# Grouped-query attention on one core: five of sixteen exps on VectorE in a fixed pattern, with three shared score slots

## The chip, the core and the metric

The kernel runs on one core of a Trainium2 chip. The metric is the device time of one execution in microseconds (us). The engines are named as in the profile: PE (TensorE, with PEld for its weight loads), ACT (ScalarE), DVE (VectorE), POOL (GpSimd), SP (SyncE, which here only issues transfers).

## What is computed

Q is (8, 512, 32, 64), K and V are (8, 512, 8, 64), all float32. Four query heads share one KV head.

```python
scale = 1.0 / np.sqrt(dim)
scores = np.einsum('bhqd,bhkd->bhqk', Q, K_expanded) * scale
weights = np.exp(scores - np.max(scores, axis=-1, keepdims=True))
weights = weights / (np.sum(weights, axis=-1, keepdims=True) + 1e-10)
output = np.einsum('bhqk,bhkd->bhqd', weights, V_expanded)
```

The kernel leaves out the subtraction of the maximum; the quotient is the same. It works on bfloat16 inputs of the matmuls.

## The kernel before, in words

*Units, pairs, tiles.* The work is cut into 32 units: one batch and two KV heads, so eight query heads. A unit has four pairs of heads (one head of each half of the 128 partitions), and a pair has four chunks of 128 keys. One score tile is 128 keys by two heads by 512 queries: two matmuls of 64 rows by 512 columns (L247, in `mm_scores`) into a PSUM slot of two banks. So a unit has 16 score tiles. The exps of the four tiles of a pair lie in one SBUF tile `pt`, of which there are four.

*Exps.* Three chunks of each pair go to ACT (L257, one activation with Exp over 128x1024, slots `sa`, two of them). The chunk with number 1 goes to DVE (L265, slot `sd`, one): a multiply and an add whose result, written as uint16, is the bit pattern of a bfloat16 near the exp. So ACT has 12 and DVE 4 of a unit's 16.

*Output.* A unit has 32 output blocks of 128 queries by 65 columns (64 of V and a column of ones that gives the sum of the weights). A block is four matmuls, one for each chunk of keys, with `pt` as the weights (L281, in `mm_out`). Four or seven blocks share one of two PSUM banks `x`; DVE copies them into `raw` in SBUF (L301, in `take_out`). After the last copy of a unit DVE takes the reciprocals (L314), POOL multiplies (L316) into `o_sb`, and POOL issues the store of 1 MB (L328).

*Turning.* K and q come in by POOL's transfers, which cast them to bfloat16 (L217, L224; V by L229). PE transposes them (L343: 4 transposes for the K of a unit, twice 8 for its q) into `x`, DVE copies them out (L350, L357). Two small transfers on SP's queue then exchange the halves of K's partitions (L351, L352, 64 KB each), since half of the score matmuls need K in the other half. POOL spreads V so that each head has its column of ones (L234, L237).

*Order.* Nothing is scheduled by the machine. A class `Plan` plays the program through with fixed costs for each kind of work and writes one list of operations; the kernel issues them in that order, engine by engine. At each step PE takes whichever of three things can start: a score for ACT, a score for DVE, or the next piece of a list of fills (output blocks and transposes in a fixed order, L361 to L372). So the scores lie singly or in twos and threes between the fills; a steady unit has 11 groups of scores and 11 groups of fills.

*Start and end.* The first unit's K and half of its q come in as float32 on SP's and ACT's queues, are cast on DVE and ACT, and turned (L395 to L433). The last unit is finished in parts: its first half and its third quarter are divided on POOL, its last quarter on DVE, and the three stores go on SP's queue.

Of the kernel before, what the change touches and what calls it, by code (L numbers as in the profile page):

```python
# [22 lines left out]
class Plan:  # L23
# [4 lines left out]

    SCORE, SCORE_LAT = 0.222, 0.436
# [5 lines left out]
    def __init__(self, npair, kcs, on_dve, fills, arrive, x_cost, nact, ndve, nx, npt, ahead, look):  # L35
        self.ops = []
        order = [(p, kc) for p in range(npair) for kc in range(kcs)]
        qa = [t for t in order if not on_dve(*t)]
        qd = [t for t in order if on_dve(*t)]
        act_free, dve_free, pt_done, pair_done = [], [], {}, {}  # L40
        parts, x_free = {(0, None): 0.0, (0, 0): 0.0}, [0.0] * nx
        ready = []
        pe = act = dve = 0.0
        ia = id_ = fi = at = nxt = 0
        slot = 0
        scoring = False

        def ring(free, issued, n):
            if issued < n:
                return 0.0  # L50
            return free[issued - n] if len(free) > issued - n else NEVER

        def score_at(q, i, free, n):
            if i >= len(q):
                return NEVER
            p = q[i][0]
            if p >= npt and p - npt not in pair_done:
                return NEVER
            u, j = divmod(p, 4)
            return max(  # L60
                ring(free, i, n), parts.get((u, None), NEVER), parts.get((u, j // 2), NEVER)
            )

        def fill_at():
            if fi >= len(fills):
                return NEVER
            f = fills[fi]
            x = x_free[nxt % nx] if at == 0 else 0.0
            if f[0] == "turn":
                return max(x, arrive(f))  # L70
            p = f[1] * 4 + (f[2] + at) // 8
            return max([x] + [pt_done.get((p, kc), NEVER) for kc in range(kcs)])

        def run_dve(until):
            nonlocal dve
            while ready:
                now = [j for j in ready if j[0] <= dve]
                j = min(now, key=lambda j: (j[1] == "score", j[0])) if now else min(
                    ready, key=lambda j: j[0]
                )  # L80
                start = max(dve, j[0])
                if start > until:
                    return
                ready.remove(j)
                self.ops.append((start, "dve", j[1], j[2]))
                if j[1] == "score":
                    cost, vis = self.SCH, self.SCH_VIS
                    dve_free.append(start + vis)
                    pt_done[j[2]] = start + vis
                else:  # L90
                    cost, vis = x_cost(j[2])
                    x_free[j[3]] = start + vis
                    if j[1] == "turn":
                        swap = 4.0 if j[2][2] is None else 0.0
                        parts[(j[2][1], j[2][2])] = start + vis + swap
                dve = start + cost

        while True:
            run_dve(pe)
            ta = score_at(qa, ia, act_free, nact)  # L100
            td = score_at(qd, id_, dve_free, ndve)
            if td < NEVER and ia < len(qa):
                p, kc = qd[id_]
                if p * kcs + kc > qa[ia][0] * kcs + qa[ia][1] + ahead:
                    td = NEVER
            tf = fill_at()
            first = min(ta, td, tf)
            if first > pe and ready:
                soon = min(max(dve, j[0]) for j in ready)
                if soon < first and ta > pe + look:  # L110
                    pe = max(pe, soon)
                    run_dve(pe)
                    continue
            if first >= NEVER:
                break
            if ta <= pe + look or (first == ta and not (scoring and td <= pe)):
                kind = "act"
            elif scoring and td <= pe:
                kind = "dve"
            elif tf <= pe or first == tf:  # L120
                kind = "fill"
            else:
                kind = "dve"
            if kind == "fill":
                f = fills[fi]
                pe = max(pe + (self.DRAIN if scoring else 0.0), tf)
                scoring = False
                self.ops.append((pe, "pe", f[0], (f, at)))
                pe += self.TURN if f[0] == "turn" else self.BLOCK
                if at == 0:  # L130
                    slot = nxt % nx
                    x_free[slot] = NEVER
                    nxt += 1
                at += 1
                if f[0] == "out" and (f[2] + at) % 8 == 0:
                    pair_done[f[1] * 4 + (f[2] + at) // 8 - 1] = pe
                if at == f[3]:
                    ready.append((pe + self.X_LAT, f[0], f, slot))
                    fi, at = fi + 1, 0
                continue  # L140
            pe = max(pe + (0.0 if scoring else self.DRAIN), ta if kind == "act" else td)
            scoring = True
            if kind == "act":
                self.ops.append((pe, "pe", "act", qa[ia]))
                start = max(act, pe + self.SCORE_LAT)
                self.ops.append((start, "act", "score", qa[ia]))
                act = start + self.EXP
                act_free.append(start + self.EXP_VIS)
                pt_done[qa[ia]] = start + self.EXP_VIS
                ia += 1  # L150
            else:
                self.ops.append((pe, "pe", "dve", qd[id_]))
                ready.append((pe + self.SCORE_LAT, "score", qd[id_], None))
                id_ += 1
            pe += self.SCORE
        assert ia == len(qa) and id_ == len(qd) and fi == len(fills) and not ready
        self.ops = [o for _, o in sorted(enumerate(self.ops), key=lambda e: (e[1][0], e[0]))]
# [3 lines left out]
def kernel(  # L161
# [15 lines left out]
    NP = NU * HPG  # L177
# [3 lines left out]
    D1 = D + 1  # L181

    scale = 1.0 / math.sqrt(D)
    DVE_KC = 1
    LOOK = 0.0
    A_schr = (2.0 ** 7) / math.log(2.0) * scale
    B_schr = 127.0 * (2.0 ** 7) - 7.35
# [9 lines left out]
    pt_pool = ctx.enter_context(tc.tile_pool(name="pt", bufs=4))  # L197
    raw_pool = ctx.enter_context(tc.tile_pool(name="raw", bufs=3))
    osb_pool = ctx.enter_context(tc.tile_pool(name="osb", bufs=3))
    inv_pool = ctx.enter_context(tc.tile_pool(name="inv", bufs=3))  # L200
    apsum = ctx.enter_context(tc.tile_pool(name="apsum", bufs=2, space=bass.MemoryType.PSUM))
    dpsum = ctx.enter_context(tc.tile_pool(name="dpsum", bufs=1, space=bass.MemoryType.PSUM))
# [5 lines left out]
    score, xs = {}, {}  # L208

# [3 lines left out]
    def load_q(u, half=None):  # L213
        b, gp = divmod(u, GP)
        lo, hi = (0, HU) if half is None else (half * HPG, (half + 1) * HPG)
        t = qn_pool.tile([128, SC, HU * D], BF16, name="q_nat")
        nc.gpsimd.dma_start(  # L217
            out=t[:, :, lo * D:hi * D], in_=rows(Q, b, HU * gp + lo, HU * gp + hi)
# [13 lines left out]
    def spread_v(b, cuts):  # L232
        t = v1_pool.tile([128, SC, KV, D1], BF16, name="v1")
        nc.gpsimd.memset(t[:, :, :, D:D1], 1.0)  # L234
        v = vn.pop(b).rearrange("p sc (h d) -> p sc h d", h=KV)
        for lo, hi in cuts:
            nc.gpsimd.tensor_copy(out=t[:, :, lo:hi, 0:D], in_=v[:, :, lo:hi, :])  # L237
        v1[b] = t

    def mm_scores(p, kc, dve):  # L240
# [3 lines left out]
        s = (dpsum if dve else apsum).tile([128, 2, S], FP32, name="sd" if dve else "sa")  # L244
# [9 lines left out]
        score[(p, kc)] = s  # L254

    def exp_act(p, kc):
        nc.scalar.activation(  # L257
            out=pts[p][:, kc, :, :],
            in_=score.pop((p, kc)),
# [4 lines left out]
    def exp_dve(p, kc):  # L264
        nc.vector.tensor_scalar(  # L265
            out=pts[p][:, kc, :, :].bitcast(U16),
            in0=score.pop((p, kc)),
            scalar1=float(A_schr),
            scalar2=float(B_schr),
            op0=mybir.AluOpType.mult,  # L270
            op1=mybir.AluOpType.add,
        )

    def mm_out(f, at):
# [5 lines left out]
        for kc in range(SC):  # L280
# [3 lines left out]
                v1[u // GP][:, kc, 2 * (u % GP) + 2 * i // HPG, :],  # L284
# [5 lines left out]
    def take_out(f):  # L290
# [5 lines left out]
        if u == NU - 1 and lo >= 3 * BLK:  # L296
            divide(u, lo, n, nc.vector, x[:, 0:n * D1].rearrange("p (n c) -> p n c", c=D1))
            if lo + n == UB:
                store(u, 3 * BLK, BLK, nc.sync)
            return  # L300
        nc.vector.tensor_copy(out=raws[u][:, lo:lo + n, :], in_=x[:, 0:n * D1])  # L301
        if u < NU - 1:
            if lo + n == UB:
                divide(u, 0, UB, nc.gpsimd)
                store(u, 0, UB, nc.gpsimd)
        elif lo + n in (2 * BLK, 3 * BLK):
            a = 0 if lo + n == 2 * BLK else 2 * BLK
            divide(u, a, lo + n - a, nc.gpsimd)
            store(u, a, lo + n - a, nc.sync)
# [35 lines left out]
    def take_turn(f):  # L345
# [8 lines left out]
        else:  # L354
# [3 lines left out]
            if part == 1 and u + 3 < NU and u >= 1:  # L358
                load_q(u + 3)
# [125 lines left out]
```

The softmax here doesn't subtract the row's maximum and nothing guards it: scores larger than these inputs give would overflow.

## Time and profile before

| | us |
|---|---|
| median of three runs | 381.35 (380.27 to 383.28) |
| the profiled execution | 384.5 |
| its span, first to last instruction | 382.6 |
| first exp on ACT starts | 8.67 |
| last exp on ACT ends | 372.3 |

The profile shows one execution. It is read by engine (busy time, share of the span, number of instructions), by groups of instructions (busy time, mean length of one in ns, idle time just before them and what ended it), by waits, and by a time line (start, length, engine, line, what is written from what). Matmuls are pipelined and the ends of their records are modelled, so a busy PE is not PE at its peak. An instruction's record can begin before the one ahead of it on its engine has ended, so the pitch of a row of instructions is shorter than the length of one.

| stretch, us | PE busy | DVE busy | ACT busy | POOL busy |
|---|---|---|---|---|
| 0 to 20 | 11.91 | 8.35 | 10.14 | 8.42 |
| 42 to 350 (308 us) | 303.59 | 260.32 | 305.25 | 162.86 |
| 372.3 to 382.6 | 1.33 | 1.77 | 0.00 | 3.23 |

### The profile page before, as it was taken

What the parts mean: (1) busy time and instruction counts of PE and PEld (TensorE: products, weight loads), DVE (VectorE), ACT (ScalarE), POOL (GpSimd) and SP (SyncE); (2) the same over time, 40 slices, a digit from 0 to 9 for tenths busy, and PEclk for the clock granted to TensorE, in tenths of its full rate; (3) what the DMA queues carried; (4) which work ended last, traced back from release to release, by engine and by line L of the source; (5) the groups of instructions that cost most, each with busy time, mean ns of one, the idle gap of its engine ahead of it and who ended that gap; (6) DMA issues with size and microseconds to landing.
All of it is one profiled execution on the core that took longest, in us unless ns stands there. A gap on an engine that the chain in (4) does not pass through costs nothing.

```text
span 382.6 us, 12995 instructions
## 1 busy us (share of the span) xinstructions
PE 359.7 (94%) x5764; PEld 226.9 (59%) x5764; DVE 305.3 (80%) x426; ACT 358.5 (94%) x387; POOL 192.3 (50%) x135
## 2 busy tenths in 40 slices
PE   3799999999999999999999999999999999999990
PEld 1355566666666666566666666666666666666660
DVE  2577788888888888888887888888888888888871
ACT  3699999999999999999999999999999999999990
POOL 5225353656545475554546555355754535444452
PEclk9999999999999999999999999999999999999997
DMA  8978776596678956599765967779566996431136
GB/s 173 208 125 145 166 181 168 144 229 155 150 167 195 251 151 149 123 223 210 182 159 144 226 137 175 173 177 253 165 128 125 229 226 172 136 121 66 66 113 219
DMA packets 41961, 64.15 MB, mean 168 GB/s; under 512 B 2352, under 2 KB 33968, under 8 KB 41904
## 3 DMA queue, kind: packets, MB, share of 16 engines
q0 software_dynamic: 33776, 57.41, 66.8%
q1 hardware_dynamic: 7600, 5.64, 5.6%
q8 instruction: 45, 0.74, 0.8%
q10 hardware_dynamic: 528, 0.26, 0.2%
q14 instruction: 12, 0.10, 0.1%
HBM read 50.59 MB, written 33.55 MB: 220 GB/s over the span
## 4 chain that ended last, share of the span: by engine, by line
PE 70%; DVE 18%; DMA 3%; issue 2%; POOL 2%; ACT 1%; POOLq 0%; ACTq 0%; DVEq 0%
PE x L281 32%; PE sa L247 23%; DVE pt L265 9%; PE x L343 9%; DVE raw L301 8%; PE sd L247 6%; DMA q_nat<-in_Q_dram 3%; ACT pt L257 1%; POOL o_sb L316 1%; POOLq L480 0%; DVE inv L314 0%; POOL v_nat L229 0%; POOL out_dram L328 0%; POOL q_nat L217 0%; POOL k_nat L224 0%
## 5 line engine op out<-in xcount | busy, mean ns | idle before, releaser
L257 ACT ACTIVATE pt<-sa 128x1024 bf16<-128x1024 f32 x384 | 356.0, 1058 | 8.9 <-PE sa L247 5.1
L281 PEld LDWEIGHTS <-pt 128*128 128x128 bf16 x4096 | 149.9, 98 | 83.3 <-issue 82.1
L316 POOL TENSOR_TENSOR o_sb<-raw,inv 128x2048 f32<-128x2048 f32 (+2 forms) x33 | 115.0, 3486 | 157.0 <-DVE inv L314 157.0
L265 DVE TENSOR_SCALAR pt<-sd 128x1024 uint16<-128x1024 f32 x128 | 154.8, 1209 | 40.6 <-PE sd L247 35.1
L247 PE MATMUL sa<-qt,kt 64*128 64x512 bf16 x768 | 150.4, 390 | 0.3 <-ACT pt L257 0.3
L301 DVE COPY raw<-x 128x455 f32<-128x455 f32 (+1 forms) x161 | 92.8, 578 | 5.7 <-PE x L281 2.7
L247 PEld LDWEIGHTS <-kt 64*128 64x128 bf16 x1024 | 44.9, 94 | 31.7 <-issue 2.4
L357 DVE COPY qt<-x 128x1024 bf16<-128x1024 bf16 x63 | 43.5, 691 | 15.1 <-PE x L343 15.1
L247 PE MATMUL sd<-qt,kt 64*128 64x512 bf16 x256 | 49.9, 386 | 0.0
L343 PE MATMUL x<-ident,q_nat 128*128 128x128 bf16 x504 | 40.4, 223 | 1.9 <-DMA q_nat<-in_Q_dram 1.9
L343 PEld LDWEIGHTS <-q_nat 128*128 128x128 bf16 x504 | 28.9, 99 | 17.5 <-issue 14.2
L217 POOL DMA_DIRECT2D q_nat<-in_Q_dram x32 | 24.0, 753 | 12.6 <-PE x L343 11.9
L328 POOL DMA_DIRECT2D out_dram<-o_sb x31 | 25.2, 813 | 9.3 <-POOL o_sb L316 9.3
L281 PE MATMUL x<-v_155,pt 128*128 128x65 bf16 x512 | 23.6, 195 | 1.4 <-DVE raw L301 1.2
L281 PE MATMUL x<-v_3756,pt 128*128 128x65 bf16 x512 | 23.1, 194 | 0.7 <-DVE raw L301 0.3
L281 PE MATMUL x<-v_2773,pt 128*128 128x65 bf16 x512 | 23.1, 194 | 0.6 <-DVE raw L301 0.3
L281 PE MATMUL x<-v_1790,pt 128*128 128x65 bf16 x512 | 23.1, 194 | 0.6 <-DVE raw L301 0.5
L281 PE MATMUL x<-v_807,pt 128*128 128x65 bf16 x512 | 23.1, 194 | 0.6 <-DVE raw L301 0.3
L281 PE MATMUL x<-v_5722,pt 128*128 128x65 bf16 x512 | 23.1, 194 | 0.6 <-DVE raw L301 0.3
L281 PE MATMUL x<-v_4739,pt 128*128 128x65 bf16 x512 | 23.1, 194 | 0.6 <-DVE raw L301 0.5
L281 PE MATMUL x<-v_6705,pt 128*128 128x65 bf16 x512 | 22.3, 194 | 0.6 <-DVE raw L301 0.3
L343 PE MATMUL x<-ident,k_nat 128*128 128x128 bf16 x124 | 17.2, 224 | 0.1
(42 smaller groups left out, 74.1 us busy)
## 6 DMA issues: line engine op xcount, KB each, us to landing
out_dram<-o_sb POOLq DMA_DIRECT2D x31, 1024.0 KB, 5.6
q_nat<-in_Q_dram POOLq DMA_DIRECT2D x31, 512.0 KB, 8.1
v_nat<-in_V_dram POOLq DMA_DIRECT2D x8, 512.0 KB, 12.5
k_nat<-in_K_dram POOLq DMA_DIRECT2D x8, 512.0 KB, 10.3
kt<-kt SPq DMA_DIRECT2D x62, 64.0 KB, 2.0
out_dram<-o_sb SPq DMA_DIRECT2D x1, 512.0 KB, 5.4
out_dram<-o_sb SPq DMA_DIRECT2D x2, 256.0 KB, 5.3
q_102<-in_Q_dram ACTq DMA_DIRECT2D x1, 256.0 KB, 4.4
```

Of the source, the lines that this page charges most:

```text
L217: nc.gpsimd.dma_start(out=t[:, :, lo * D:hi * D], in_=rows(Q, b, HU * gp + lo, HU * gp + hi))
L247: nc.tensor.matmul(s[:, m, :], kt[u][64 * m:64 * m + 64, 0 if m == g else 1, kc * 128:(kc + 1) * 128], qt[u][64 * m:64 * m + 64, i, :], st ...
L257: nc.scalar.activation(out=pts[p][:, kc, :, :], in_=score.pop((p, kc)), func=mybir.ActivationFunctionType.Exp, scale=float(scale),)
L265: nc.vector.tensor_scalar(out=pts[p][:, kc, :, :].bitcast(U16), in0=score.pop((p, kc)), scalar1=float(A_schr), scalar2=float(B_schr), op0= ...
L281: nc.tensor.matmul(xs[f][:, at * D1:(at + 1) * D1], pts[u * HPG + i][:, kc, m, qc * 128:(qc + 1) * 128], v1[u // GP][:, kc, 2 * (u % GP) + ...
L301: nc.vector.tensor_copy(out=raws[u][:, lo:lo + n, :], in_=x[:, 0:n * D1])
L316: eng.tensor_tensor(out=osbs[u].rearrange("p qc h d -> p h qc d")[:, lo // SC:lo // SC + nh], in0=src[:, :, 0:D].rearrange("p (h qc) d -> ...
L328: eng.dma_start(out=rows(out, b, HU * gp + h0, HU * gp + h1), in_=osbs[u][:, :, h0:h1, :].rearrange("p qc h d -> p qc (h d)"),)
L343: nc.tensor.transpose(xs[f][:, at * 128:(at + 1) * 128], src, ident)
L357: nc.vector.tensor_copy(out=qt[u][:, 2 * part:2 * part + 2, :], in_=x)
```

## The change

The order is no longer chosen step by step. A fixed pattern for a unit names, score by score, whether the next tile is one for ACT or for DVE, and how many fills follow it:

- 11 of a unit's 16 exps go to ACT and five to DVE. The scores come as ACT, DVE, ACT five times and then one for ACT; after each third score, and after the last, come 12, 10, 8, 7, 11 and 4 fills (a fill is a transpose or an output block).
- The three score slots in PSUM are shared by both engines: a score takes the one that comes free first by the plan. Their size in PSUM is as before.
- Of the five tiles on DVE, four are made as before. The fifth (tile 7 of a unit) is made in three steps: DVE writes bit patterns with another constant into a tile `lo`; POOL adds 64 to each, which is half an octave in a bfloat16, into `hi`; POOL adds the two as bfloat16 into `pt`.
- There are six `pt` tiles instead of four. The output groups of a unit have 7, 4, 7, 7 and 7 blocks, with q's and K's transposes between them.
- Stores are issued from SP's queue, by the plan's clock some time after the division was issued on POOL. The last unit's last two stores are one for each four blocks, on ACT's and SP's queues, and its third quarter is divided on DVE.
- At the start, ten matmuls on zeros are put ahead; the two forms of K are turned one after the other, and q's second part after the first two scores; the first unit's V comes in as float32 on SP's queue and is spread on POOL, and the rest of V is loaded after q and K. V's spread for the next batch is asked for at the same place as before in the units, with its tiles kept by unit.

The core of the diff, without most of the planner:

```diff
+        for u in range(nu + 3):
+            for k in range(16):
+                at_dve = scores[k] == "D"
...
+                    while True:
+                        s = min(range(nslot), key=lambda i: slots[i])
...
+                    self.pe = max(start, slots[s])
...
+                carry += fill[k]
...
+                while carry > 0 and gi < len(groups):
...
+    TILES = [int(c) for c in "0100010201000100"]
+    SCORES = "ADAADAADAADAADAA"
+    FILL = [0, 0, 12, 0, 0, 10, 0, 0, 8, 0, 0, 7, 0, 0, 11, 4]
+    ORDER = "08 o7 o4 18 o7 K4 o7 o7".split()
+    SKIP = 9
...
-    B_schr = 127.0 * (2.0 ** 7) - 7.35
+    B_one = 127.0 * (2.0 ** 7) - 7.35
+    B_two = 127.0 * (2.0 ** 7) - 170.25
+    HALF_OCTAVE = 64
...
-    pt_pool = ctx.enter_context(tc.tile_pool(name="pt", bufs=4))
+    pt_pool = ctx.enter_context(tc.tile_pool(name="pt", bufs=6))
+    two_pool = ctx.enter_context(tc.tile_pool(name="two", bufs=2))
...
-    apsum = ctx.enter_context(tc.tile_pool(name="apsum", bufs=2, space=bass.MemoryType.PSUM))
-    dpsum = ctx.enter_context(tc.tile_pool(name="dpsum", bufs=1, space=bass.MemoryType.PSUM))
+    spsum = ctx.enter_context(tc.tile_pool(name="spsum", bufs=1, space=bass.MemoryType.PSUM))
...
-        s = (dpsum if dve else apsum).tile([128, 2, S], FP32, name="sd" if dve else "sa")
+        s = spsum.tile([128, 2, S], FP32, name=f"s{slot}")
...
+        two = TILES[t % len(TILES)] == 2
+        dst = pts[p][:, kc, :, :]
+        bits = two_pool.tile([128, 2, S], U16, name="lo") if two else dst.bitcast(U16)
         nc.vector.tensor_scalar(
-            out=pts[p][:, kc, :, :].bitcast(U16),
-            in0=score.pop((p, kc)),
+            out=bits,
+            in0=score.pop(t),
             scalar1=float(A_schr),
-            scalar2=float(B_schr),
+            scalar2=float(B_two if two else B_one),
...
+        if two:
+            high = two_pool.tile([128, 2, S], U16, name="hi")
+            nc.gpsimd.tensor_scalar(
+                out=high, in0=bits, scalar1=HALF_OCTAVE, scalar2=None, op0=mybir.AluOpType.add
+            )
+            nc.gpsimd.tensor_tensor(
+                out=dst, in0=bits.bitcast(BF16), in1=high.bitcast(BF16), op=mybir.AluOpType.add
+            )
...
-            if lo + n == UB:
-                divide(u, 0, UB, nc.gpsimd)
-                store(u, 0, UB, nc.gpsimd)
...
+            if lo < b <= lo + n:
+                divide(u, a, b - a, nc.vector if last and a else nc.gpsimd)
+                wait = 4.5 if b - a == UB else 2.8
+                later.append((now + wait, lambda a=a, b=b: store(u, a, b - a, nc.sync)))
...
+        nc.sync.dma_start(out=v32, in_=rows(V, 0, 0, 2))
+        nc.vector.memset(warm, 0.0)
...
+        load_q(0, lo=HPG)
         load_k(0)
         load_q(1)
-        load_q(2)
-        load_q(3)
...
+        for _ in range(10):
+            nc.tensor.matmul(xw, warm[:, 0:128], warm, start=True, stop=True)
...
+        turn_first(k16[:, :, 0, :], nc.vector.tensor_copy, kt[0][:, 0, :])
+        turn_first(q16[:, :, 0:2 * D], nc.scalar.copy, qt[0][:, 0, :])
+        turn_first(k16[:, :, 1, :], nc.vector.tensor_copy, kt[0][:, 1, :])
```

## The prediction

> **What bounds the kernel now.** I read the engine shares first, then the groups of instructions, then the time line of one steady unit (one batch, two KV heads; 32 in all), and last the waits and the DMA landings. The shares and the costliest groups:
>
> ```profile
> PE 359.7 (94%) x5764; PEld 226.9 (59%) x5764; DVE 305.3 (80%) x426; ACT 358.5 (94%) x387; POOL 192.3 (50%) x135
> ...
> L257 ACT ACTIVATE pt<-sa 128x1024 bf16<-128x1024 f32 x384 | 356.0, 1058 | 8.9 <-PE sa L247 5.1
> ...
> L316 POOL TENSOR_TENSOR o_sb<-raw,inv 128x2048 f32<-128x2048 f32 (+2 forms) x33 | 115.0, 3486 | 157.0 <-DVE inv L314 157.0
> L265 DVE TENSOR_SCALAR pt<-sd 128x1024 uint16<-128x1024 f32 x128 | 154.8, 1209 | 40.6 <-PE sd L247 35.1
> ```
>
> ACT and PE are both at 94%, and ACT idles 8.9 us in all. ACT exps overlap: 1058 ns is one exp's length, not its pitch. The time line of ACT gives the pitch:
>
> ```profile
> 13.33 2.85 ACT L257 ACTIVATE pt<-sa 128x1024 bf16<-128x1024 f32 x3 [1.80 <-PE sa L247]
> 17.45 1.02 ACT L257 ACTIVATE pt<-sa 128x1024 bf16<-128x1024 f32 x1 [1.26 <-PE sa L247]
> ...
> 41.73 165.20 ACT L257 ACTIVATE pt<-sa 128x1024 bf16<-128x1024 f32 x177 [0.36 <-ACT pt L257]
> ```
>
> Unhindered, three exps take 2.85 us, so the pitch is (2.85 - 1.02)/2 = 0.915 us; in the long stretch it is (165.20 - 1.06)/176 = 0.933. Twelve exps a unit are 10.98 us unhindered and 11.20 as they run. The same 11.20 stands between the equal copies of two units on DVE (186.57 and 197.77). Next, PE and DVE in such a unit:
>
> ```profile
> 186.90 0.54 PEld L247 LDWEIGHTS <-kt 64*128 64x128 bf16 x6
> 187.66 0.91 PEld L281 LDWEIGHTS <-pt 128*128 128x128 bf16 x28 [0.23 <-issue]
> 188.62 0.10 PEld L247 LDWEIGHTS <-kt 64*128 64x128 bf16 x2
> 188.94 0.18 PEld L281 LDWEIGHTS <-pt 128*128 128x128 bf16 x4 [0.23 <-issue]
> 189.17 0.29 PEld L247 LDWEIGHTS <-kt 64*128 64x128 bf16 x4
> ...
> 195.82 1.22 DVE L265 TENSOR_SCALAR pt<-sd 128x1024 uint16<-128x1024 f32 x1 [0.17 <-ACT pt L257]
> 196.96 0.62 DVE L301 COPY raw<-x 128x455 f32<-128x455 f32 x1
> 197.77 0.69 DVE L357 COPY qt<-x 128x1024 bf16<-128x1024 bf16 x1 [0.19 <-PE x L343]
> ```
>
> Three score tiles in a row hold PE 0.76 us (186.90 to 187.66), one alone 0.32; 28 output matmuls (7 blocks) hold it 0.96, 4 (one block) 0.23. So a score is 0.22 plus 0.10 for the change of kind, a fill 0.11 plus 0.122 a block, and a transpose 0.056 (8 in 0.45). Before, a unit has 11 score groups and 11 fills: 16 x 0.22 + 11 x 0.10 + 11 x 0.11 + 32 x 0.122 + 20 x 0.056 = 10.9 us. PE at 10.9 and ACT at 11.0 share the bound; their hand-overs make it 11.20. DVE has room:
>
> ```profile
> 186.60:197.80 11.20, 11.05 (x186) 7.04 (x183) 9.49 (x14) 11.11 (x13) 5.17 (x3) 1.00 0.64 151
> ```
>
> Its columns are PE, PEld, DVE, ACT, POOL, clock, DMA share, GB/s: DVE 9.49 of 11.20, POOL 5.17 (6.0 on average). PE runs at full clock.
>
> **The change part by part, per steady unit.**
>
> *ACT*: 11 exps instead of 12, 11 x 0.915 = 10.07 us.
>
> *PE*: the same 16 scores, 32 blocks and 20 transposes, but the scores come as five triplets (ACT, DVE, ACT) and one single. Six score groups, 5 x 0.76 + 0.32 = 4.12; six fills, 6 x 0.11 + 3.90 + 1.12 = 5.68. Together 9.80, 1.1 less than before.
>
> *DVE*: a fifth exp. An instruction that follows directly starts 0.08 early (1.22 then 1.14 to the next start). Packed: exps 5 x 1.14, 7-block copies 4 x 0.55, 4-block copy 0.34, q copies 2 x 0.61, k copy 0.34, reciprocal 0.27 = 10.07 us. With as little overlap as now, the busy time alone is 9.49 + 1.14 = 10.6.
>
> So three engines end within 0.3 us of each other, and hand-overs decide. I walk one unit by hand. Of a triplet beginning at a, the DVE exp starts at a + 0.22 + 0.49 (195.33 to 195.82 in the time line) and frees its slot 1.30 later; the written-out order leaves DVE one slot and ACT two within a unit. The second ACT score needs the slot of the exp before the one just fed, so the triplet takes 0.84 instead of 0.76. Behind it stand the fills of 1.05 (4 blocks, 8 transposes), 1.13 (7 and 3), 1.02 (7 and 1), 0.96 (7) and 0.93 (3 and 8): triplets of 1.89, 1.97, 1.86, 1.80, 1.77, and the single with 4 blocks 0.92. Sum 10.21. DVE's exps start 0.75, 0.90, 0.71, 0.88 and 1.04 into them, because the copies of 4 blocks and q, of k and 7 blocks, and the reciprocal stand ahead; the fourth holds its slot about 0.16 past the next score, and PE, in order, waits with all behind it. That makes 10.37. Before, 10.98 of ACT became 11.20; part of such a loss is already in the walk, so I add 0.13 and take **10.5 us**. Its bounds: 10.07 (nothing waits) and 11.2 (all gained is lost again).
>
> *POOL*: new are an add over 128x1024 uint16 and a sum of two 128x1024 bf16. Neither is in the trace. The nearest rows:
>
> ```profile
> L316 POOL TENSOR_TENSOR o_sb<-raw,inv 128x1024 f32<-128x1024 f32 x1 | 1.9, 1912 | 0.0
> ...
> L237 POOL COPY v_155<-v_nat 128x1536 bf16<-128x1536 bf16 x1 | 1.5, 1472 | 0.0
> ```
>
> For the sum I take 1.9 us (same shape and inputs, wider type), for the add 1.05 (the copies, 1.472 for 1536 and 1.907 for 2048, scaled). Bounds of the pair: 2.1 (two copies) and 7.2 (each as long as the 3.62 us division). POOL's unit: 3.62 + 0.75 for the q load + (0.75 + 0.78 + 0.26 + 1.91)/4 for K, V and its spreading = 5.3; the store's 0.81 goes to SP; with 3.0 it is 8.3, hidden below 10.5. In the order the pair stands ahead of the division, and behind it the division, the store (SP) and the next q load wait: about 3 us later each, covered by three output buffers and a q tile loaded three units ahead. The pair feeds block 8 of the next unit's output; from the third triplet's exp to there I count 5.5 us, so 3.0 is covered; beyond 5.5 PE waits, and with it every score behind that block.
>
> *SP*: the store now waits in SP's queue for the division, ahead of the next two K swaps.
>
> ```profile
> DMA to landing us min/median/max: 1.9/2.0/5.5
> ```
>
> That is the swap, alone in its queue; the stores, nearly all from POOL, landed in 4.6 to 6.8 us. The store starts about 7.1 us after the fourth triplet begins, the swap 10.8 after, and the first score that needs it is at 15.0. With the store's slowest 6.8 us it ends at 13.9: no charge; the bounds are 0 and, if every swap took its worst 5.5 us from the end of its issue at 11.9, 17.4 - 15.0 = 2.4 us a unit. I take 0: the median swap is the nearest row.
>
> The Trainium skill, DMA: Bandwidth & Descriptors, section Queues, rings and completion order, speaks against this move: SP's transfers share one ring on each DMA engine, consumed in order, so a swap cannot overtake the megabyte ahead of it. By this rule the swap lands some 2 us behind the store: with the median store still before 15.0, with the slowest near 15.9, which would put up to 32 x 0.9 = 29 us on the sum; by the row nothing is added. No run here shows a large store ahead of a swap on that queue.
>
> *Buffers, constants, slicing of V1*: no instruction in the steady unit; nothing.
>
> *Start*: ACT's first exp is at 8.67 and it idles 4.7 more before 41.7. The first eight K transposes took 1.20 us where later ones take 0.62, though the granted clock reads 1.00 throughout; ten matmuls on zeros now run ahead of them (early score pairs start 0.40 apart, so about 4 us, over near 5.3, when K's transposes now begin at 5.17); K is turned in halves; the other half of q is loaded ahead of V (issue 0.92). Against it, V's spread comes late and the first add and sum stand behind it. I take -2 us, bounds -4 and +2.
>
> *Tail*: from the last exp to the end are 10.3 us. The third quarter's division moves to DVE, which waited 0.8 for POOL, and the last two stores go on two queues; but 96 instead of 72 output matmuls follow the last score (+0.8). I take 0, bounds -1.5 and +1.5.
>
> *Sum*: 32 x (11.20 - 10.5) = 22.4, with the start 24.4. The profiled execution took 384.5 (span 382.6, 1.9 around it): 360.1. The median of the runs shown lies 3.15 under that execution, so the forecast is **357 us**. Its own range (10.3 to 10.7 a unit, start and tail by their bounds) is 350 to 365.
>
> **The rivals.**
>
> *DVE's queue becomes the bound* (faster, less). For it: DVE idles 40.6 us ahead of its 128 exps now, 0.32 each, because each waits for its own score; if a unit is 10.6 busy plus 0.3 of such waits, it is 10.9, saving 9.6 and 2: about 370. Against it: in the walk copies fill those gaps.
>
> *GpSimd is too slow* (slower). Point of decision: the pair above 5.2 us makes POOL the bound at 10.5, above 5.9 the unit exceeds 11.2. At 6.5 the unit is 11.8: 381.35 + 32 x 0.6 - 2 = 399; at 7.2 it is 12.5, 421. For it: integers on POOL have no row. Against it: both nearest rows give half.
>
> *The K swap behind the store* (slower or nothing gained): 0.7 a unit lost eats the gain, about 379; needs landings past 15.7.
>
> **How the numbers follow.** Chances: the forecast 0.62, the DVE queue 0.2, swap or other stalls that leave nothing 0.05, GpSimd too slow, or stalls past 0.8 us a unit, 0.13. About 1% is what a measurement of this kernel can tell from none (377.5 to 385.2): faster 0.82, same 0.05, slower 0.13. The range 349 to 374 holds the first case and most of the second, leaving 0.2 outside.
>
> **What would show it.** Equal DVE copies 10.5 us apart; ACT's mean pitch near 0.95; POOL's two new rows near 1.05 and 1.9; no wait of the first score of a unit for the swap; few waits of PE for POOL. Wrong, if PE's scores wait for DVE's exp more than 0.5 us a unit, or POOL is above 90% busy.

## The result, and the profile after

The changed kernel takes 407.52 us (median of four, 401.26 to 415.94) against 381.72 of the kernel before. The ratio is 1.057, 95% interval 1.044 to 1.070; it goes by the two faster executions (401.26 and 406.05), because those more than 1.5% above the fastest are left out. Forecast were 357. The profiled execution is the slowest of the four (415.94 us, span 414.2), so its waits may be longer than those of the others.

The page of the changed kernel, with the lines that answer to those shown of before:

```profile
span 414.2 us, 13144 instructions
PE 360.5 (87%) x5774; PEld 234.5 (57%) x5774; DVE 336.3 (81%) x462; ACT 336.1 (81%) x355; POOL 323.3 (78%) x169
...
L287 POOL TENSOR_SCALAR hi<-lo 128x1024 uint16<-128x1024 uint16 x32 | 88.8, 2774 | 68.6 <-DVE lo L277 66.5
...
L290 POOL TENSOR_TENSOR pt<-lo,hi 128x1024 bf16<-128x1024 bf16 x32 | 68.0, 2124 | 2.7
...
kt<-kt SPq DMA_DIRECT2D x62, 64.0 KB, 5.4
```

No engine is busy above 87%, so none is the bound. POOL's add takes 2.77 us and its sum 2.12. K's swap lands 5.4 us after its issue (median), where it took 2.0 before. The waits of PE and PEld of the same kernel (total, times, longest):

```profile
PEld L254 <- DMA kt<-kt: 40.6, 21, 4.7
...
PE s_6078 L254 <- DMA kt<-kt: 4.4, 1, 4.4
...
PE s_1583 L254 <- DMA kt<-kt: 3.3, 1, 3.3
```

PEld and PE wait at the same time here (the weights are K), so they are not added. PE's own waits for the swap, listed score by score, sum to about 34 us. One of them in the time line:

```profile
200.51 0.38 SPq L347 DMA_DIRECT2D out_dram<-o_sb  x1
202.33 0.83 POOL L222 DMA_DIRECT2D q_nat<-in_Q_dram  x1
202.65 0.46 SPq L370 DMA_DIRECT2D kt<-kt  x1
203.15 0.61 SPq L371 DMA_DIRECT2D kt<-kt  x1
...
208.25 0.33 PEld L254 LDWEIGHTS <-kt 64*128 64x128 bf16 x5 [1.33 <-DMA kt<-kt]
208.26 0.39 PE L254 MATMUL s_4080<-qt,kt 64*128 64x512 bf16 x1 [1.04 <-DMA kt<-kt]
...
208.73 1.02 ACT L265 ACTIVATE pt<-s_4080 128x1024 bf16<-128x1024 f32 x1 [1.18 <-issue]
```

The store goes out at 200.51, the q load at 202.33, the swap at 202.65 and 203.15. By the landings in the trace the store is done at 204.72, the second swap at 208.59 and the q load at 209.88. The score that needs the swap stands first in a unit, so PE stands still, and with it ACT and DVE, which wait for PE's scores.

A wait has a second price. Stretches around a longer one; the columns are PE, PEld, DVE, ACT, POOL, then the granted clock of PE, the DMA share, GB/s:

```profile
178.00:180.70 2.70, 2.69 (x43) 1.68 (x40) 2.67 (x5) 2.62 (x4) 2.62 (x2) 1.00 1.14 190
180.70:183.80 3.10, 0.00 (x0) 0.00 (x0) 0.34 (x1) 0.33 (x1) 3.10 (x2) 0.79 1.22 217
183.80:186.00 2.20, 2.16 (x20) 1.05 (x21) 1.02 (x1) 1.47 (x2) 1.68 (x2) 0.50 1.25 207
186.00:188.00 2.00, 2.00 (x20) 1.16 (x17) 1.33 (x3) 0.74 (x2) 0.00 (x0) 0.50 1.14 311
188.00:190.00 2.00, 2.00 (x37) 1.43 (x35) 1.32 (x2) 1.66 (x2) 0.00 (x0) 0.67 1.10 344
190.00:196.00 6.00, 5.95 (x105) 3.88 (x105) 5.89 (x9) 5.53 (x6) 3.98 (x2) 1.00 0.54 101
```

PE is idle for 3.1 us, and 1.8 us into that its clock falls to half (at 182.50 in the trace). It runs at half for another 5.5 us: 20 matmuls in 2 us, and in the worst stretch ACT is fed 0.74 us of 2. The Trainium skill, TensorE: Matmul & The Clock Gate, Part 1, has a rule for this: an idle window of about 3.4 us brings half the rate until a busy window has passed. The row shows the half rate, but it came after 1.8 us without a matmul, sooner than the rule has it.

Where no swap is late, near the end of the same execution, units last 10.7 and 10.4 us at the full clock:

```profile
358.10:368.80 10.70, 10.60 (x183) 6.97 (x180) 10.29 (x14) 10.40 (x11) 8.79 (x5) 1.00 0.36 120
368.80:379.20 10.40, 10.31 (x181) 7.01 (x180) 10.10 (x14) 10.22 (x11) 8.21 (x4) 1.00 0.34 117
```

So in these units the pattern does what was forecast of it. That the whole loss lies in the late swaps is what the experiments have to show.

### The profile page after: what moved, and what is told of

Same layout as the page of the kernel before. It is cut to its first block, busy times and chain, and to the rows that moved or that the text cites. A ratio compares the mean times of both kernels' runs of the same rounds, so it can differ in the third digit from the quotient of the medians.

```text
span 414.2 us, 13144 instructions
## 1 busy us (share of the span) xinstructions
PE 360.5 (87%) x5774; PEld 234.5 (57%) x5774; DVE 336.3 (81%) x462; ACT 336.1 (81%) x355; POOL 323.3 (78%) x169
## 4 chain that ended last, share of the span: by engine, by line
PE 40%; DMA 32%; DVE 11%; issue 8%; ACT 5%; POOL 3%; SPq 0%; ACTq 0%; DVEq 0%; POOLq 0%
DMA kt<-kt 28%; PE x L301 17%; DVE pt L277 5%; PE x L362 5%; ACT pt L265 5%; DMA q_nat<-in_Q_dram 3%; DVE raw L321 2%; DVE kt L369 2%; POOL hi L287 1%; DMA v_104<-in_V_dram 1%; DVE lo L277 1%; POOL pt L290 1%; DVE qt L376 1%; POOL o_sb L335 0%; DVE inv L333 0%
## 5 line engine op out<-in xcount | busy, mean ns | idle before, releaser
L301 PEld LDWEIGHTS <-pt 128*128 128x128 bf16 x4096 | 144.9, 100 | 41.6 <-issue 39.6
L287 POOL TENSOR_SCALAR hi<-lo 128x1024 uint16<-128x1024 uint16 x32 | 88.8, 2774 | 68.6 <-DVE lo L277 66.5
L335 POOL TENSOR_TENSOR o_sb<-raw,inv 128x2048 f32<-128x2048 f32 (+1 forms) x33 | 114.1, 3459 | 3.1 <-DVE inv L333 3.1
L254 PEld LDWEIGHTS <-kt 64*128 64x128 bf16 x1024 | 55.0, 95 | 107.6 <-DMA kt<-kt 40.6
L290 POOL TENSOR_TENSOR pt<-lo,hi 128x1024 bf16<-128x1024 bf16 x32 | 68.0, 2124 | 2.7
L362 PEld LDWEIGHTS <-q_nat 128*128 128x128 bf16 x504 | 31.4, 103 | 10.1 <-issue 7.7
L301 PE MATMUL x<-v_6825,pt 128*128 128x65 bf16 x512 | 21.3, 203 | 1.9 <-POOL pt L290 1.9
L301 PE MATMUL x<-v_4827,pt 128*128 128x65 bf16 x512 | 20.9, 199 | 0.0
L301 PE MATMUL x<-v_1830,pt 128*128 128x65 bf16 x512 | 20.7, 198 | 0.0
L301 PE MATMUL x<-v_5826,pt 128*128 128x65 bf16 x512 | 20.6, 198 | 0.0
L301 PE MATMUL x<-v_831,pt 128*128 128x65 bf16 x512 | 20.5, 197 | 0.0
L301 PE MATMUL x<-v_2829,pt 128*128 128x65 bf16 x512 | 20.4, 197 | 0.0
L301 PE MATMUL x<-v_3828,pt 128*128 128x65 bf16 x512 | 19.7, 194 | 0.0
L362 PE MATMUL x<-ident,k_nat 128*128 128x128 bf16 x124 | 17.2, 222 | 0.0
L301 PE MATMUL x<-v_182,pt 128*128 128x65 bf16 x384 | 15.1, 196 | 0.0
L362 PEld LDWEIGHTS <-k_nat 128*128 128x128 bf16 x124 | 8.7, 97 | 8.9 <-issue 8.9
L369 DVE COPY kt<-x 128x512 bf16<-128x512 bf16 x31 | 12.9, 415 | 0.0
L333 DVE RECIPROCAL inv<-raw 128x32 f32<-128x32 f32 (+2 forms) x34 | 11.6, 340 | 1.3
## 6 DMA issues: line engine op xcount, KB each, us to landing
v_nat<-in_V_dram POOLq DMA_DIRECT2D x8, 512.0 KB, 12.8
```

The lines of the kernel that those rows point to most:

```text
L254: nc.tensor.matmul(s[:, m, :], kt[u][64 * m:64 * m + 64, 0 if m == g else 1, kc * 128:(kc + 1) * 128], qt[u][64 * m:64 * m + 64, i, :], st ...
L287: nc.gpsimd.tensor_scalar(out=high, in0=bits, scalar1=HALF_OCTAVE, scalar2=None, op0=mybir.AluOpType.add)
L290: nc.gpsimd.tensor_tensor(out=dst, in0=bits.bitcast(BF16), in1=high.bitcast(BF16), op=mybir.AluOpType.add)
L301: nc.tensor.matmul(xs[f][:, at * D1:(at + 1) * D1], pts[u * HPG + i][:, kc, m, qc * 128:(qc + 1) * 128], v1[u][:, kc, 2 * i // HPG, :], st ...
L335: eng.tensor_tensor(out=osbs[u].rearrange("p qc h d -> p h qc d")[:, lo // SC:lo // SC + nh], in0=src[:, :, 0:D].rearrange("p (h qc) d -> ...
L362: nc.tensor.transpose(xs[f][:, at * 128:(at + 1) * 128], src, ident)
```

## The experiments

The theory after the result, A: the swap lands late, and PE waits for it. At first it was A1: in SP's queue the swap lies behind the store. Against it B: POOL's pair makes POOL the bound. And C: the pattern of scores does not hold. All ratios are to the kernel before, with 95% intervals.

**One value instead of two.** POOL's add and sum are left out, so the fifth tile is the cruder value.

```diff
-    TILES = [int(c) for c in "0100010201000100"]
+    TILES = [int(c) for c in "0100010101000100"]
```

> The changed kernel with the fifth DVE tile made like the other four: one value in place of the sum of two, so POOL's add and sum are left out. Theory A (K's swap lies behind the store in SP's queue and PE waits for it): the division starts about 5 us earlier, the store ends before the swap is issued, PE's waits for the swap go from about 40 us to under 5, and the time is about 360 us (31 units of 10.5, a first unit of about 15, 7.4 before it and 12.5 behind). Theory B (POOL's pair of 4.9 us is itself the bound, 10.2 us of a unit): the same fall, to about 360. Theory C (the pattern of scores does not hold 10.5 us a unit): still over 375.

Measured: 375.96 us, ratio 0.981 (0.976 to 0.985). A and B missed. C's number came (over 375), but not its cause: units without a late swap take 10.4 us. The store now leaves about 5 us earlier, but PE still waits 14.7 us in 13 waits for the swap, which lands in 4.2 us (median). In six of the 13 the store has less than 0.8 us to go when the swap is issued, and what stays on its way is the q load; in the seven others K and V are loading. That speaks against A1 as the whole cause.

**The store on POOL's queue.**

```diff
-                later.append((now + wait, lambda a=a, b=b: store(u, a, b - a, nc.sync)))
+                later.append((now + wait, lambda a=a, b=b: store(u, a, b - a, nc.gpsimd if b - a == UB else nc.sync)))
```

> The changed kernel with the 1 MB stores issued from POOL's queue as before, so that the swap is alone in SP's queue. A: the swap lands in about 2 us again, no wait of PE for it is left; POOL's unit becomes 10.2 + 0.8 = 11.0 us, so the time is at most about 379 us, and 361 if POOL still keeps up. B: POOL has more to do, so no gain: 405 us or more. C: over 375 with the swap's wait gone and POOL below 90% busy.

Measured: 420.88 us, ratio 1.095 (1.087 to 1.102). The landing of the swap, alone in SP's queue but for the end of the kernel:

```profile
DMA to landing us min/median/max: 2.0/5.7/8.7
```

A1 as the whole cause falls: with no store ahead of it in its queue the swap lands no sooner, and PE's waits for it are 35.0 us. The time is what B gave (405 or more), but POOL is at 83%, and the next run rules B out.

A2 takes its place: the swap is slow while other large transfers are on the same DMA engines, whatever queue they came by. I sorted the swaps of each trace by what else was in flight between the first issue of a pair and its second landing (pairs, and the median of that time in us). A transfer counts if it shared more than 0.9 us of that time; pairs beside other mixtures are left out, 4 of 31 in the first row and 9 in each of the others:

| kernel | nothing else | store | store and q | K and V too |
|---|---|---|---|---|
| before | 14: 2.5 | 6: 3.6 | 1: 4.1 | 6: 5.7 |
| changed | | 3: 4.3 | 14: 6.0 | 5: 8.0 |
| store on POOL | | 3: 4.9 | 15: 7.6 | 4: 8.3 |

The kernel before already had slow swaps, when K and V were loading. There nobody waited. (Its column "store" proves nothing: its store always left 2.0 us after the swap's first issue, so a pair stands there because it was slow. In the two other rows the store and the q load mostly left before the swap.) That the DMA engines are the part of the path that is shared is not shown by these counts; they show that the queue does not decide.

**K turned a unit earlier.** The swap keeps its traffic, but has a unit to land.

```diff
-    SKIP = 9
+    SKIP = 5
...
+    groups += [("turn", 2, None, 4)]
...
+            elif kind == "K":
+                if u + 3 < NU:
+                    groups.append(("turn", u + 3, None, n))
             elif u + 2 < NU:
-                groups.append(("turn", u + 2, None if kind == "K" else int(kind), n))
+                groups.append(("turn", u + 2, int(kind), n))
...
+                if r == 8 and b + 1 < B:
+                    load_k(b + 1)
                 if r == 24 and b + 1 < B:
-                    load_k(b + 1)
                     load_v(b + 1)
```

> The changed kernel with K turned (and swapped) one unit earlier and its load issued 16 score tiles earlier; the store stays on SP's queue and POOL's work is unchanged. A: the swap still lands in about 5 us but nobody waits for it; about 361 us. B: POOL's work and the store's time are as in the changed kernel, so about 400 us. C: over 375 with no wait for the swap.

Measured: 364.49 us, ratio 0.952 (0.947 to 0.956). The landing of the swap in this kernel, its engine shares, and 27 units from its fourth on:

```profile
DMA to landing us min/median/max: 2.1/6.2/8.4
...
PE 340.5 (94%) x5774; PEld 226.0 (62%) x5774; DVE 335.2 (92%) x462; ACT 335.2 (92%) x355; POOL 323.8 (89%) x169
...
42.90:326.40 283.50, 279.12 (x4864) 188.08 (x4860) 279.35 (x379) 280.54 (x298) 270.82 (x133) 1.00 0.82 185
```

The swap is slower than ever, and no wait for it is left among PE's. From its third unit on, all but one and the last take 10.4 to 10.7 us (10.5 on average in the stretch shown, at the full clock), though POOL is at 89%. A holds, B and C fall. Start and tail are less than 2 us shorter than in the changed kernel, so nearly all of the difference between 407.5 and 364.5 us is the wait for the swap and the half clock behind it.

**The add as an int32 sum.** The 1024 uint16 of a row are added as 512 words with a constant tile of 64 x 65537.

```diff
-            nc.gpsimd.tensor_scalar(
-                out=high, in0=bits, scalar1=HALF_OCTAVE, scalar2=None, op0=mybir.AluOpType.add
-            )
+            nc.gpsimd.tensor_tensor(
+                out=high.bitcast(I32), in0=bits.bitcast(I32), in1=consts["step"], op=mybir.AluOpType.add
+            )
...
```

> The changed kernel with POOL's add of 64 over 1024 uint16 done as an int32 sum of 512 words with a constant tile. The float division of 1024 took 1.9 us, so 512 words should take about 1.1 instead of 2.77, and POOL's pair 3.2 instead of 4.9. A: the division and the store come 1.7 us earlier, so of the waits for the swap (1 to 4.7 us each) most of the length goes: 365 to 380 us. B: POOL falls to 8.5 us a unit, about 361. C: over 375.

Measured: 384.80 us, ratio 1.004 (1.001 to 1.008). The add fell from 2.77 to 1.26 us, and PE's waits for the swap from 34 to 16.6 us. The direction is A's, but 365 to 380 was expected of it; the size was less, because the swap still met the store and the q load in 10 pairs, and K and V as well in six more.

**Which transfer?** Three kernels move the other transfers away from the swap. First the q load, asked for when K is copied out instead of when q is, so that POOL issues it before the division:

```diff
             kt[u] = k
+            if 2 <= u and u + 3 < NU:
+                load_q(u + 3)
...
-            if turned[u] == 2 and 1 <= u and u + 3 < NU:
+            if turned[u] == 2 and 1 == u:
```

> The changed kernel with the next unit's q load issued on POOL ahead of the division instead of behind it, about 5 us earlier, so that it is nearly over when the swap is issued; the store stays as in the changed kernel. A2 (the swap is slow because other large transfers are in flight on the same DMA engines, whatever queue they came by), with q as the larger part: the swap lands in about 3 us, few waits, about 366 us. A2 with the store as the larger part, or A1 (the swap cannot overtake the store in SP's queue): landings stay near 5 us, about 400 us.

Measured: 393.54 us, ratio 1.027 (1.020 to 1.034); median landing 4.1 us, PE's waits 21.8. Between the two values: some of the traffic was gone. Then the store behind the swap:

```diff
-                wait = 4.5 if b - a == UB else 2.8
+                wait = 9.5 if b - a == UB else 2.8
```

> The changed kernel with the store placed behind the swap in SP's order, so that no store is ahead of the swap in its queue; q's load stays as in the changed kernel. A1, or A2 with the store as the larger part: the swap lands in 2 to 3 us, about 362 to 366 us. A2 with the q load as the larger part: landings stay near 5 us, about 395 us.

Measured: 394.75 us (386.89 to 395.74, too far apart for a ratio); median landing 4.6 us, PE's waits 20.2. Nothing is ahead of the swap in its queue now, and it is still slow with q in flight: A1 as the whole cause falls once more, and neither transfer alone is the cause. Then both edits:

> The changed kernel with both: q's load ahead of the division and the store behind the swap, so that the swap meets only the end of the q load. A1 and A2: landings of 2 to 3 us, no wait of PE for the swap, 361 to 365 us. If the swap is slow for another reason (its own size, or the K and V loads), the waits stay and the time is over 380.

Measured: 379.62 us, ratio 0.992 (0.988 to 0.996). The landing of the swap:

```profile
DMA to landing us min/median/max: 1.9/2.2/7.6
```

The median is near that of the kernel before (2.0). The rest, 12.9 us of waits, is the third theory of its expectation, though the time came just under the 380 that it gave: all seven stand in every fourth unit, where K and V load. The six pairs beside store, q, K and V took 7.4 us, the 18 with the store alone 2.6. (A store issued behind the swap hardly slows it.)

Split in this way, the three runs say more than their medians. In the units where K and V do not load, PE's waits for the swap are 18.9 us in the changed kernel, 1.7 with q first, 4.8 with the store late and 0 with both. So there it takes the store and the q load together to make PE wait for long. In the units where K and V load they are 15.5, 20.1, 15.4 and 12.9 us: none of the three kernels cures those. (Each is read from one execution.)

**K early and the int32 sum.** Both edits together.

> K turned a unit earlier, and POOL's add as an int32 sum of 512 words (pair of 3.4 us instead of 4.9). If the unit of 10.47 us is set by PE, ACT and DVE alone, POOL's 1.5 us less a unit change nothing but the start: 361 to 365 us. If POOL at 97% of a unit still holds the others up (its unit is about 10.2), the unit falls to 10.3 or less: 355 to 360.

Measured: 359.92 us, ratio 0.944 (0.939 to 0.949), the fastest here and faster than both kernels. Engine shares and a row of the page, then a stretch of four units:

```profile
PE 337.5 (94%) x5774; PEld 224.4 (63%) x5774; DVE 335.2 (94%) x463; ACT 335.2 (94%) x355; POOL 274.1 (77%) x169
```

```profile
84.00:126.00 42.00, 41.45 (x722) 27.86 (x721) 41.22 (x57) 41.77 (x45) 34.21 (x21) 1.00 0.86 190
```

The time lies at the upper end of the second range (355 to 360), but the unit, which that theory put at 10.3 or less, stays at 10.46 us: POOL does not set it. PE, DVE and ACT are all above 98% in it. Against K early alone, 1.8 us are won in the first two units and 2.3 in the tail (12.1 to 9.8), where the pair stands ahead of output matmuls that have no unit of slack.

**Four exps on DVE in this version.** Tile 7 goes to ACT.

```diff
-    TILES = [int(c) for c in "0100010201000100"]
-    SCORES = "ADAADAADAADAADAA"
+    TILES = [int(c) for c in "0100010001000100"]
+    SCORES = "ADAADAAAADAADAAA"
```

> K turned a unit early and the same pattern, but tile 7 goes to ACT in the place of DVE: twelve exps on ACT, four on DVE, no pair on POOL. If the gain of the version with the int32 sum (360 us) comes from the fifth exp, ACT is the bound again with 12 exps of 0.904 to 0.92, 10.9 to 11.0 us a unit instead of 10.47: 360 + 32 x 0.45 = 374 us. If the pattern, the start and the tail brought it, the time stays near 360.

Measured: 387.00 us, ratio 1.013 (1.006 to 1.020). A unit lasts 11.50 us, more than either theory gave. The waits of PE:

```profile
PE s L256 <- ACT pt L267: 32.0, 93, 0.7
```

The third triplet is now three ACT scores in a row; PE waits for a slot in each unit, up to 0.7 us, and one exp of a unit starts 1.26 us after the one ahead of it, where most start 0.90 to 0.92 apart. So this pattern with four exps on DVE brings nothing against the order before, and the fifth exp brings 27 us to it (387.0 to 359.9). A better place for the twelfth ACT exp was not tried.

**The start.** In the version with K early and the int32 sum, the third unit's q is loaded ahead of V.

```diff
         load_q(1)
+        load_q(2)
...
         load_v(0)
-        load_q(2)
         load_q(3)
```

> K turned a unit early, the int32 sum, and at the start the load of the third unit's q asked for ahead of V's, since a transpose waits 1.9 us for it at 18.5 us. If that wait sets the start: 357 to 358 us. If V's spread, which comes later by it, is late next: 360 or more.

Measured: 364.69 us, ratio 0.954 (0.949 to 0.959): 4.8 us worse than without. Time lines of POOL and PE:

```profile
18.64 1.89 POOL L242 COPY v<-v_nat 128x2048 bf16<-128x2048 bf16 x1 [9.38 <-DMA v_nat<-in_V_dram]
20.47 0.74 POOL L231 DMA_DIRECT2D k_nat<-in_K_dram  x1
21.23 1.27 POOL L289 TENSOR_TENSOR hi<-lo,step 128x512 int32<-128x512 int32 x1
22.58 2.12 POOL L292 TENSOR_TENSOR pt<-lo,hi 128x1024 bf16<-128x1024 bf16 x1
```

```profile
24.75 0.68 PE L303 MATMUL x<-v1f,pt 128*128 128x65 bf16 x9 [4.68 <-POOL pt L292]
```

V lands later, POOL waits 9.4 us for it with the add and the sum queued behind, and PE waits 4.7 for the sum. As the second case of the expectation has it, V's spread was late next, and with it the pair behind it.

## Why the prediction was wrong, point by point

- *The unit without disturbance, 10.5 us.* Right: 10.46 in the best version, 10.4 to 10.7 in quiet units of the changed kernel. The walk came out right as a sum; its terms were not measured one by one, and 0.13 of it was a guess.
- *DVE's queue becomes the bound (370).* It did not: DVE is above 98% busy in a quiet unit, but so are PE and ACT, and the unit holds at 10.46.
- *POOL's pair, 3.0 us.* Mis-sized: 4.9 (the sum 2.12 for 1.9, the add 2.77 for 1.05), inside the bounds of 2.1 and 7.2. POOL's unit is then about 10.2, still below the unit, so the rival with GpSimd as the bound did not come. But the division, and with it the store and the q load, came later: the store 8.8 us after the fourth triplet (191.73 to 200.51) instead of 7.1.
- *The swap, "I take 0: the median swap is the nearest row".* This step failed. A wait that was put at nothing came to about 34 us on PE, 1.1 a unit, and more at half clock behind it. The median of 2.0 came from swaps with little else in flight, and the change put the store and the q load into flight with them. The right row was the other end of the same line, 5.5 us, which belongs to the swaps beside K and V; the median is now 5.4. The upper bound of 2.4 us a unit held as an average (51.6 us against K early are 1.6 a unit), though single units took up to 17.2 us. The rival was named, with its place and its point of decision, but only as a gain lost (0.05); stalls that make the kernel slower stood with GpSimd in the 0.13.

  Nor was the rival's mechanism the one that counted. The Trainium skill, DMA: Bandwidth & Descriptors, section Issuing engines are not separate DMA queues, has a better one: transfers of all queues run on the same 16 DMA engines and interleave. The store on POOL's queue agrees, at 5.7 us. The rule on ring order, which I had weighed, does not set the delay here: 47 swaps of the changed kernel were issued with a store ahead of them in flight, and they landed almost 4 us after that store (median). (None landed before it, which is as the rule has it; with the store on POOL's queue three of 47 did.)
- *The q load, "about 3 us later each, covered".* Its own landing was covered; that it met the swap was not thought of. A moved transfer was priced by who waits for it, and not by what it slows.
- *Start, -2.* The first exp begins 1.2 us earlier (7.45 for 8.67), but the first two units lose 6.2 us against quiet ones, where the first three lost 4.9 before: 13.6 us of start in both. K early has 12.2 and the best version 10.6 (7.91 and 2.7), so the term was there to be had, but not with the swap late and the add slow. One reading was wrong: the granted clock was taken as 1.00 throughout. The trace of the kernel before has no entry for the clock ahead of 19.62 us, and up to there the two matmuls of a score take 0.61 us, from there on 0.39. With the ten matmuls on zeros ahead, they take 0.39 from 8.1 us on.
- *Tail, 0 with a bound of +1.5.* 12.5 us against 10.3, beyond the bound: PE waits 1.9 us for the last unit's sum on POOL. With the faster add it is 9.8, and in the two versions without POOL's pair 6.0, so the pair in the last unit is a cost that the prediction did not see. And the last unit itself, which had no term, is longer than the others: 12.8 us for 10.5 in the best version, where before it took 11.2. In that version's time line:

```profile
335.71 2.99 PE L303 MATMUL x<-v,pt 128*128 128x65 bf16 x92
...
339.06 2.85 ACT L267 ACTIVATE pt<-s 128x1024 bf16<-128x1024 f32 x3 [1.90 <-PE s L256]
```

92 output matmuls run in a row between two scores, where the same time line has at most 28 between 100 and 112 us, and ACT waits 1.9 us.

- *The range, 350 to 365.* It is not the plain sum of its bounds, which gives 347 to 369.

How the 51.6 us between the spans of the changed kernel and of the one with K early divide was not tried apart. An estimate from the two profiles: PE waits 34 us for the swap, and it is busy 360.5 us instead of 340.5 with the same 5774 matmuls; together 54. In the changed kernel its clock is at 0.50 for 41 us in seven stretches between 59 and 340 us, with K early never between 23 and 350. So the slow clock cost some half as much again as the waits themselves.

## What to carry to other kernels

A small transfer that something waits for is to be priced with whatever will be in flight beside it, on any queue: take its slowest landings in the trace, and see what was in flight in them. When a change moves a large transfer, ask not only who waits for it but which small one it now meets; the cheap cure is to ask for the small one earlier. A stall of 2 or 3 us can cost half as much again, if PE's clock falls behind it.

## What the runs showed of the hardware that was not expected

- The 64 KB swap takes 2.5 us for a pair of issues with nothing else in flight, 6.0 to 7.6 (medians of two kernels) beside a 1 MB store and a 0.5 MB q load, and up to 9 beside K and V as well, with the store on the same queue or on another.
- On GpSimd an add of a constant to 1024 uint16 takes 2.77 us, more than the sum of two bf16 tiles of 1024 (2.12) or the multiplication of two f32 ones (1.90). As 512 int32 words with a constant tile it takes 1.26.
- PE's granted clock fell to 0.50 after 1.8 us without a matmul (180.7 to 182.5 in the changed kernel) and stayed there for 6.8 us; in the kernel with the int32 sum alone it fell after 1.6 us (165.4 to 167.0), for 3.4. Other pauses of up to 2.6 us did not bring it down, so no threshold can be read from these runs.
